# A mixture-of-experts kernel on one core: weight loads in units of 4 MB over groups of four slots, and one shared scatter for the last two experts

## The chip, the core and the metric

The kernel runs on one NeuronCore of a Trainium2 chip. Five engines work from queues of their own and meet through semaphores: TensorE (PE, matrix products), VectorE (DVE), ScalarE (ACT), GpSimd (POOL) and SyncE (SP, which here only issues transfers). 16 DMA engines move data between HBM and the on-chip memory SBUF. Each engine takes its instructions strictly in the order of its queue: an instruction that waits holds up all that stand behind it. The metric is the device time of one execution in microseconds, lower is better.

## The reference

One decoder layer on 256 tokens of width 1024, in float32: a mixer (a Mamba-2 branch and a gated MLP branch), cross-attention into 256 memory tokens, and a mixture of experts, each followed by a residual layer norm. The mixture of experts is what the change is about. The router picks 4 of 32 experts for each token; then for every expert

```
hgu  = xt @ w_gu[e] + b_gu[e]                 # 1024 x 2048 weights, 8 MB
gate = min(hgu[:, :1024], 7); up = clip(hgu[:, 1024:], -7, 7)
y    = ((up + 1) * gate * sigmoid(1.702 * gate)) @ w_down[e] + b_down[e]   # 1024 x 1024, 4 MB
acc += gates[:, e] * y
```

The weights of the experts are 32 x 12 MB = 384 MB, and each is read once.

## The kernel before

Phase A (mixer and attention) takes 20 or so slots of 1 MB in SBUF for its weights and intermediates. In phase B the experts follow one another, two experts to a pair. An expert takes at most 64 tokens. `gather` picks the tokens of a pair with a one-hot matrix (tile `pair`) into `xg` (a part of `cd`): four gathers per pair, each 8 matmuls into a PSUM buffer `sm` and two copies out, the first on ACT, the second on DVE. `gate_up` multiplies them with the 8 row blocks k of `w_gu` (eight instructions per k in the trace, four in the program) into two PSUM tiles `gu`, adds the bias with four short matmuls (line 1057) and then computes SwiGLU: DVE takes the minimum `gc` (line 1062), ACT the sigmoid `sg` (1063), DVE the clip (1064), the product (1065) and the last product `uc` (1066). `hidden_t` transposes `uc` by four matmuls (1075) into `sm`, and ACT copies the result to `hT` (1076). `down` multiplies `hT` with `w_down` (1089). After each odd expert `scatter` adds the weighted rows of the pair to `acc` (1100, 1105). PSUM tiles named `sm` have two buffers, which gathers, transposes, gate weights and scatters share.

What is issued when: the text of the kernel starts expert e+1 (its row blocks 0 and 1, `AHEAD = 2`) before the transposes of expert e. That is a wish, not the order: the instructions are put in order, engine by engine, by a scheduler at build time which estimates when each one's data will be there and takes what it holds to be ready first. So a change in the loads can change the order of the matmuls.

The weights of the experts come through SP's queue. `expert_w` gives each unit of the stream its slots: the first 22 loads of 1 MB go to slots as phase A gives them up (`FIRST`), then a ring of ten double slots (`RING`) takes units of 2 MB, of which a row (one partition's part) is 16384 bytes. A load waits until the matmuls that read its slots before are done. At the most 8 transfers are under way, since there are 8 semaphores for them.

At e = 14, 16 and 20 three pieces of other work are put between the experts: a table of overfull experts, `add_rest` (residual and bias rows, which also loads two small tiles `bd` through SP's queue) and the last norm's factors. At the end the last expert goes by column pieces: `scatter_one` adds expert 30 by itself (1116), then four `down_piece` (1124) with a `scatter_piece` each (1133) run for expert 31 with weights of its own (`weights_solo`), and `finish` normalizes and stores.

Of the kernel before, what the change touches and what calls it, by code (L numbers as in the profile page):

```python
# [8 lines left out]
F32 = mybir.dt.float32  # L9
# [8 lines left out]
P = 128  # L18
# [31 lines left out]
def block_kernel(ctx: ExitStack, tc: tile.TileContext, a, out):  # L50
# [11 lines left out]

    arena = cp.tile([P, len(SLOTS), 2048], F32, name="arena")
    big = ctx.enter_context(tc.tile_pool(name="big", bufs=1))

    def two(tag, dt=F32):

        return big.tile([P, 2, 2048], dt, tag=tag, name=uniq(tag))

# [133 lines left out]
    def w_parts():  # L203
        t = two(("t01", "t23")[tcount[0] % 2], F32R).rearrange("p q (i c) -> p q i c", i=2)
        tcount[0] += 1
        return [[t[:, q, i] for q in range(2)] for i in range(2)]
# [122 lines left out]
    kT = bt("e0").rearrange("p (k m) -> p k m", k=KB)  # L329
    mh, ml = feat("ab")  # L330
    hs, ls = w_parts()
# [30 lines left out]
    keys(2, wk2)  # L362
    xh, xl = feat("xhl")
    for k2 in range(4):
# [18 lines left out]

    gbm = bt("g").rearrange("p (g d) -> p g d", g=2)
    gvu = two("ab")
    gv = gvu[:, 0].rearrange("p (c d) -> p c d", c=2)
    st = stats_tile(2)
# [18 lines left out]
    ygh, ygl = feat("cd")  # L406
    uT = gvu[:, 1].rearrange("p (k t) -> p k t", k=KB)

# [190 lines left out]

    ysh, ysl = feat("ab")  # L600

# [79 lines left out]
    x1 = bt("h").rearrange("p (c d) -> p c d", c=2)  # L681
    mh, ml = feat("ab")
    mem = []
# [11 lines left out]
    proj_residual(hh, hl, x0, x1, st)  # L695
    xh, xl = feat("xhl")
    bg3 = bgs[:96, :].bitcast(BF16)
# [255 lines left out]
    class Pair:  # L953
# [36 lines left out]

        def weights_solo(self):

            G = self.gated()
            G2 = wk.tile([P, 2, 2, 2, CAP], F32, tag="t2", name="G2")
            pt = pst("sm", 2).rearrange("p (r c t) -> p r c t", r=2, c=2)
            for i in range(2):
                for c in range(2):
                    ve.tensor_copy(G2[:, i, c], G[:, c, i:i + 1, :].to_broadcast([P, 2, CAP]))
                    te.transpose(pt[:, i, c, :], G2[:, i, c].rearrange("p b s -> p (b s)"), ident)
            t = wk.tile([P, 2, 2, P], F32, tag="uy", name="PS")  # L1000
            se.activation(t, pt, AF.Copy)
            return [t[:, i] for i in range(2)]

    ucount = [0]

    def expert_w(src, apart=False):

        i = ucount[0]
        ucount[0] += 1
        if 2 * i < len(FIRST):  # L1010
            t = []
            for h in range(2):
                name = FIRST[2 * i + h]
                with tc.issue_after(wload[PHASE_A.index(FIRST_AFTER.get(name, ("wo", 3)))].ins):
                    if name in SLOTS:
                        t.append(bt(name))
                    elif name == "d":
                        t.append(cd[:, 1])
                    else:
                        if h == 0:  # L1020
                            both = two(name)
                        t.append(both[:, h])
                    nc.sync.dma_start(t[h], src[:, h])
            return t
        name = RING[(i - len(FIRST) // 2) % len(RING)]
        if name in SLOTS:
            at = SLOTS.index(name)
            t = arena[:, at:at + 2, :]
        else:
            t = two(name)  # L1030
        if apart:
            for h in range(2):
                nc.sync.dma_start(t[:, h], src[:, h])
        else:
            nc.sync.dma_start(t, src)
        return [t[:, h] for h in range(2)]

    def gate_up(src, sel, xe, before=None, last=False):

# [38 lines left out]

    def down(src, odd, hT, y, apart=False, between=None):

        for u in range(2):
            if u and between is not None:
                between()
            w = expert_w(src(u), apart)
            for b in range(4):
                k = 4 * u + b
                for n in range(2):
                    o = 64 * (n ^ odd)
                    te.matmul(y[n][o:o + 64, :], hT[:, b, 64 * u:64 * u + 64],  # L1089
                              w[b // 2][:, b % 2 * D + n * 512:b % 2 * D + (n + 1) * 512], start=(k == 0), stop=(k == KB - 1))  # L1090

# [14 lines left out]

    def scatter_one(y, PT):

        ys = wk.tile([P, 512], F32, tag="ux", name=uniq("ys"))
        se.activation(ys[0:64, :], y[0][0:64, :], AF.Copy)  # L1110
        ve.tensor_copy(ys[64:128, :], y[1][64:128, :])
        for n in range(2):
            o = slice(64 * n, 64 * n + 64)
            for c in range(2):
                ps = pst("sm", 2)
                te.matmul(ps, PT[o, c, :], ys[o, :], start=True, stop=True)
                av = acc[:, c, n * 512:(n + 1) * 512]
                ve.tensor_tensor(av, ps, av, ALU.add)

    def down_piece(hT, w, q):  # L1120
# [5 lines left out]
        ys = wk.tile([P, 512], F32, tag="ux", name=uniq("ys"))[:, :256]  # L1126
        se.activation(ys, y, AF.Copy)
        return ys

    def scatter_piece(ys, PT, q, st):  # L1130
        for c in range(2):
            ps = pst("sm", 2)[:, :256]
            te.matmul(ps, PT[:, c, :], ys, start=True, stop=True)
# [32 lines left out]
    def before(e, k):  # L1166
# [10 lines left out]
        if e % 2 and k % 2 == 0 and e < NE - 1:  # L1177
            pairs[e // 2 + 1].gather(k // 2)
        if e % 2 and k == 5 and e < NE - 1:
            p.weights()  # L1180

    def begin(e):
        xg = pairs[e // 2].xg
        current[e] = gate_up(lambda u: a["w_gu"][e, u], i96[:, e:e + 1], lambda k: xg[:, k, e % 2 * CAP:(e % 2 + 1) * CAP],
                             lambda k: before(e, k), e == NE - 1)

# [3 lines left out]
    for e in range(NE - 2):  # L1190
# [15 lines left out]
        if b == 0:  # L1206
            y = [pst(f"y{n}", 1) for n in range(2)]
        down(lambda u: a["w_down"][e, u], b, hT, y)
        if b:
# [10 lines left out]
    hT = hidden_t(uc)  # L1220
    PS = pairs[ea // 2].weights_solo()
    for k in range(AHEAD, KB):
# [3 lines left out]
    hTb = []  # L1226
    down(lambda u: a["w_down"][ea, u], 0, hT, y, True, lambda: hTb.append(hidden_t(uc)))
    scatter_one(y, PS[0])
    ys = None
    for q in range(4):  # L1230
        if q % 2 == 0:
            w = expert_w(a["w_last"][q // 2], True)
        new = down_piece(hTb[0], w[q % 2], q)
        if ys is not None:
            scatter_piece(ys, PS[1], q - 1, st)
        ys = new
    scatter_piece(ys, PS[1], 3, st)
    finish(st)
# [3 lines left out]
    with tc.For_i(0, nx, 1):  # L1242
# [35 lines left out]
        hT = hidden_t(swiglu())  # L1278
        down(lambda u: a["w_down"][bass.ds(ev, 1), u].rearrange("e p h d -> p (e h) d"), 0, hT, y)
        ys = wk.tile([P, 512], F32, tag="ux", name="ysx")  # L1280
# [11 lines left out]
        for i in range(2):  # L1292
# [8 lines left out]

FIRST = ["e1", "k", "g", "gb", "xhl", "xhl", "w3", "w4", "e0", "x0", "ab", "ab", "w5", "w0", "w1", "w2", "t01", "t01", "t23",
         "t23", "j", "d"]
SLOTS = ["e1", "k", "g", "gb", "w3", "w4", "e0", "x0", "w5", "w0", "w1", "w2", "j", "h"]
FIRST_AFTER = {"e1": ("z", 1), "k": ("wq", 0), "g": ("wq", 1), "gb": ("wo", 0)}

RING = FIRST[0:20:2]

# [15 lines left out]
def arrange(inputs):  # L1324
# [30 lines left out]
    wg, wd = I["w_gu"][0], I["w_down"][0]  # L1355
    r["w_gu"] = wg.reshape(NE, 4, 2, P, 2 * D).transpose(0, 1, 3, 2, 4)
    r["w_down"] = wd.reshape(NE, 2, 4, P, D).transpose(0, 1, 3, 2, 4).reshape(NE, 2, P, 2, 2 * D)
    r["w_last"] = wd[NE - 1].reshape(KB, P, 4, 256).transpose(2, 1, 0, 3).reshape(2, 2, P, 2 * D).transpose(0, 2, 1, 3)
    r["b_gu"], r["b_down"] = I["b_gu"][0], I["b_down"][0]
# [21 lines left out]
```

## Time and profile before

| | |
|---|---|
| median of 3 runs | 1318.44 us (1317.88 to 1318.74) |
| profiled execution | 1318.8 us, of which the span of its instructions 1317.1 us |
| PE busy | 1254.6 us (95%), DVE 451.4 us, ACT 315.6 us |
| read from HBM | 469.49 MB |
| first matmul of an expert | 393.62 us after the span's start |
| mean granted TensorE clock | 0.987 of full speed |

The profile page cuts the span into 40 slices of 33 us. A busy digit of 9 on PE says that matmuls were under way, not that they were dense. In the list of costliest groups and in the timelines `[2.08 <-DMA x]` says that the engine sat idle for 2.08 us before this group and that the landing of x ended it. A pair of experts is recognised by its scatter (line 1100); the time from one scatter to the next is what a pair costs.

### The profile page before, as it was taken

How to read it: one execution, taken by the hardware profiler on the slowest of the kernel's cores; microseconds unless marked ns; L12 is line 12 of the kernel's file. 1: busy time of each engine (PE TensorE's matmuls, PEld its weight loads, DVE VectorE, ACT ScalarE, POOL GpSimd, SP SyncE). 2: the span in 40 equal slices, each digit the busy share in tenths (PEclk: the TensorE clock that was granted, in tenths of full speed). 3: DMA queues.
4: the chain of work that ended last, by engine and by line, in shares of the span. 5: the costliest groups of instructions: out<-in, count | busy, mean ns of one | idle time of the engine just before them, and what ended most of it. 6: DMA issues, size and time to landing. Idle time of an engine off the chain costs nothing.

```text
span 1317.1 us, 15917 instructions
## 1 busy us (share of the span) xinstructions
PE 1254.6 (95%) x6767; PEld 686.7 (52%) x6768; DVE 451.4 (34%) x795; ACT 315.6 (24%) x536; POOL 28.6 (2%) x49
## 2 busy tenths in 40 slices
PE   6999999999999999999999999999999999989896
PEld 6899899989874343343333433333343433323232
DVE  4569766687441222121221122221221212202114
ACT  4746665544531111111111111101111111101000
POOL 2110000001000000000000000000000000000000
PEclk9999999999999999999999999969999999999998
DMA  9755543576789999999999999999999999999993
GB/s 356 242 175 195 192 160 133 193 289 225 277 315 362 422 425 428 427 427 428 427 427 428 429 428 427 412 427 427 426 429 428 427 428 426 427 427 428 429 421 134
DMA packets 43930, 472.00 MB, mean 358 GB/s; under 512 B 5104, under 2 KB 6928, under 8 KB 10064
## 3 DMA queue, kind: packets, MB, share of 16 engines
q1 hardware_dynamic: 39840, 464.41, 85.8%
q10 hardware_dynamic: 4016, 6.55, 1.6%
q8 instruction: 54, 0.88, 0.3%
q14 instruction: 20, 0.16, 0.0%
HBM read 469.49 MB, written 1.05 MB: 357 GB/s over the span
## 4 chain that ended last, share of the span: by engine, by line
PE 78%; DMA 15%; DVE 3%; ACT 2%; issue 1%; POOL 0%; ACTq 0%; DVEq 0%; SPq 0%; POOLq 0%
PE gu L1050 27%; PE y L1089 14%; PE mm L255 6%; PE mm L239 5%; PE mm L238 5%; PE mm L237 5%; PE sm L971 4%; PE sm L1100 4%; DMA arena<-in_w_down_dram 3%; DMA arena<-in_w_gu_dram 3%; DMA ab<-in_w_gu_dram 3%; DMA t<-in_w_gu_dram 3%; DMA t<-in_w_down_dram 2%; PE sm L1075 1%; DVE t L181 1%
## 5 line engine op out<-in xcount | busy, mean ns | idle before, releaser
L1050 PE MATMUL gu<-arena,cd 128*64 128x512 f32 x1240 | 279.8, 594 | 4.5 <-DMA arena<-in_w_gu_dram 4.5
L1050 PEld LDWEIGHTS gu<-arena,cd 128*64 128x64 f32 x1240 | 86.6, 137 | 171.2 <-issue 157.4
L181 DVE TENSOR_TENSOR t<-arena,t 128x1024 fp32r<-128x1024 f32 (+1 forms) x111 | 131.9, 1210 | 49.6 <-ACT t L180 49.6
L1089 PE MATMUL y<-arena,hT 128*64 128x512 f32 x592 | 140.4, 615 | 5.6 <-ACT hT L1076 5.6
L180 ACT ACTIVATE t<-arena 128x1024 fp32r<-128x1024 f32 (+1 forms) x114 | 113.9, 1039 | 59.1 <-issue 18.5
L1062 DVE TENSOR_SCALAR gc<-gu 128x512 f32<-128x512 f32 x32 | 22.1, 692 | 297.3 <-PE gu L1057 297.3
L237 PE MATMUL mm<-xhl,t 128*128 128x256 f32 x384 | 110.5, 288 | 0.0
L239 PE MATMUL mm<-xhl,t 128*128 128x256 f32 x384 | 108.9, 283 | 1.5 <-DVE t L181 1.5
L238 PE MATMUL mm<-xhl,t 128*128 128x256 f32 x384 | 108.7, 283 | 0.0
L1063 ACT ACTIVATE sg<-gc 128x512 f32<-128x512 f32 x32 | 20.2, 630 | 341.7 <-DVE gc L1062 341.7
L975 DVE TENSOR_SCALAR cd<-sm,par 128x128 f32<-128x128 f32 x64 | 26.2, 410 | 210.5 <-ACT cd L973 210.2
L1105 DVE TENSOR_TENSOR cd<-sm,cd 128x512 f32<-128x512 f32 x56 | 38.7, 692 | 170.9 <-PE sm L1100 170.9
L1050 PE MATMUL gu<-t,cd 128*64 128x512 f32 x384 | 87.1, 595 | 0.0
L1089 PEld LDWEIGHTS y<-arena,hT 128*64 128x64 f32 x592 | 42.5, 140 | 84.4 <-issue 74.8
L973 ACT ACTIVATE cd<-sm,par 128x128 f32<-128x128 f32 x64 | 29.3, 457 | 227.4 <-PE sm L971 226.0
L971 PEld LDWEIGHTS sm<-pair,arena 128*128 128x128 f32 x512 | 62.0, 191 | 31.7 <-issue 27.2
L239 PEld LDWEIGHTS mm<-xhl,t 128*128 128x128 f32 x384 | 73.5, 192 | 1.7 <-DVE t L181 1.7
L971 PE MATMUL sm<-pair,arena 128*128 128x128 f32 x512 | 71.3, 285 | 3.2 <-ACT pair L989 1.8
L238 PEld LDWEIGHTS mm<-xhl,t 128*128 128x128 f32 x384 | 73.6, 192 | 0.2
L237 PEld LDWEIGHTS mm<-xhl,t 128*128 128x128 f32 x384 | 73.5, 192 | 0.2
L1100 PE MATMUL sm<-ys,pair 128*128 128x512 f32 x120 | 59.1, 615 | 10.4 <-ACT ys L1094 10.2
L1050 PE MATMUL gu<-ab,cd 128*64 128x512 f32 x208 | 48.8, 613 | 4.0 <-DMA ab<-in_w_gu_dram 4.0
(320 smaller groups left out, 1432.6 us busy)
## 6 DMA issues: line engine op xcount, KB each, us to landing
arena<-in_w_gu_dram SPq DMA_DIRECT2D x71, 2048.0 KB, 32.3
arena<-in_w_down_dram SPq DMA_DIRECT2D x35, 2048.0 KB, 30.2
arena<-in_wa_dram SPq DMA_DIRECT2D x56, 1024.0 KB, 5.0
t<-in_w_gu_dram SPq DMA_DIRECT2D x22, 2048.0 KB, 35.1
ab<-in_w_gu_dram SPq DMA_DIRECT2D x13, 2048.0 KB, 31.5
xhl<-in_w_gu_dram SPq DMA_DIRECT2D x12, 2048.0 KB, 30.1
t<-in_w_down_dram SPq DMA_DIRECT2D x12, 2048.0 KB, 30.9
arena<-in_w_gu_dram SPq DMA_DIRECT2D x13, 1024.0 KB, 7.3
```

The lines of the kernel that those rows point to most:

```text
L180: se.activation(h, src, AF.Copy)
L181: sub_op[0] = (eng or ve).tensor_tensor(l, src, h.bitcast(F32), ALU.subtract)
L237: te.matmul(ps[:, b, :], wh, xh[:, k, :], start=(k == 0), stop=False)
L238: te.matmul(ps[:, b, :], wh, xl[:, k, :], start=False, stop=False)
L239: te.matmul(ps[:, b, :], wl, xh[:, k, :], start=False, stop=(k == KB - 1))
L255: last[0] = te.matmul(res[c], x[:, k, c * P:(c + 1) * P], w[k // 2 % 2][:, k % 2, :], start=(k == 0 and i == 0), stop=(k == KB - 1 and i = ...
L971: te.matmul(pg[:, b, :], x2[:, c, k * P:(k + 1) * P], self.t[:, 0, c, :], start=(c == 0), stop=(c == 1))
L973: se.activation(self.xg[:, k, :], pg[:, 0, :], AF.Identity, bias=b2[:, k:k + 1], scale=g2[:, k:k + 1])
L1050: te.matmul(t[64 * j:64 * j + 64, :], xe(k), ws[k][:, n * D + j * 512:n * D + (j + 1) * 512], start=(k == 0), stop=False)
L1089: te.matmul(y[n][o:o + 64, :], hT[:, b, 64 * u:64 * u + 64], w[b // 2][:, b % 2 * D + n * 512:b % 2 * D + (n + 1) * 512], start=(k == 0), ...
L1100: te.matmul(ps, PT[:, c, :], ys[n], start=True, stop=True)
L1105: ve.tensor_tensor(av, ps, av, ALU.add)
```

## The change

Three things are altered. First the slots: eight of the one-megabyte slots that phase A uses as pairs (`xh`, `xl`, `a`, `b` and `t0` to `t3`) become two tiles of four, two intermediates of phase A move to other slots (`h` and `j`), and the order of the first slots and of the ring changes so that the ring is five groups of four. Second the units: from expert 4 on a load brings four slots at once (4 MB, rows of 32768 bytes); experts 0 to 3 keep 2 MB, the last expert's second half of `w_gu` and expert 30's `w_down` come in units of 2 MB, the last `w_down` in four of 1 MB. The first half of the next expert's `w_gu` is now asked for as one unit. Third the end: `scatter_one` and `weights_solo` go; the pieces of expert 31 are written into the upper half of the tile `ys` that holds expert 30's rows in its lower half (ACT copies one half of the PSUM piece, DVE adds the other), and one `scatter_piece` per column piece serves both experts.

```
-RING = FIRST[0:20:2]
+RING = [8, 0, 12, 4, 16]
+NRING = 4 * len(RING)
...
+    def expert_w(src, n=1):
+        out = []
+        h = src.shape[1]
+        while len(out) < h:
+            i = ucount[0]
+            if i < len(FIRST):
+                m, name = 1, FIRST[i]
...
+            else:
+                m = min(n, h - len(out))
+                at = (rcount[0] + NRING - len(FIRST) % 4) % NRING
+                rcount[0] += m
+                t = slots(RING[at // 4] + at % 4, m)
+            ucount[0] += m
+            with after:
+                nc.sync.dma_start(t, src[:, len(out):len(out) + m])
...
-            if k % 2 == 0:
-                ws[k], ws[k + 1] = expert_w(src(k // 2), last and k == KB - 2)
+            if k % 4 == 0:
+                ws.update(enumerate(expert_w(src(k // 4), n_rows[k // 4]), k))
...
-    def down(src, odd, hT, y, apart=False, between=None):
+    def down(src, odd, hT, y, rows=4, between=None):
+        w = expert_w(src, rows)
+        for k in range(KB):
+            if k == 4 and between is not None:
                 between()
...
-        se.activation(ys, y, AF.Copy)
-        return ys
+        t = ys[q // 2][64:128, q % 2 * 256:q % 2 * 256 + 256]
+        se.activation(t, y[0:64, :], AF.Copy)
+        ve.tensor_tensor(t, y[64:128, :], t, ALU.add)
...
+    def rows_of(e):
+        return (2, 2) if e < 4 else (4, 4)
...
-    PS = pairs[ea // 2].weights_solo()
-    scatter_one(y, PS[0])
+    ve.tensor_copy(ys[0][0:64, :], y[0][0:64, :])
+    se.activation(ys[1][0:64, :], y[1][64:128, :], AF.Copy)
+    PT = pairs[ea // 2].PT
+    w = expert_w(a["w_last"])
```

PE's order around the SwiGLU of an odd expert (here 27) in the kernel before: the last bias matmul (1057), two row blocks of the next expert's gate-up, the four transposes of `uc`, the first matmul of `down`.

```order
L1057 MATMUL gu_6749<-bgs,i_109 64x512
L1050 MATMUL gu_6862<-ab_6864,cd_3791 64x512 x2
L1050 MATMUL gu_6863<-ab_6864,cd_3791 64x512 x2
L1050 MATMUL gu_6862<-ab_6864,cd_3791 64x512 x2
L1050 MATMUL gu_6863<-ab_6864,cd_3791 64x512 x2
L1075 MATMUL sm_6875<-ident,uc_6856 128x128 x4
L1089 MATMUL y_14_6774<-arena,hT_6874 64x512
```

The same place in the changed kernel (lines 1055, 1048, 1073 and 1085 are those matmuls; expert 25):

```order
L1055 MATMUL gu_6359<-bgs,i_109 64x512
L1073 MATMUL sm_6479<-ident,uc_6461 128x128
L1048 MATMUL gu_6467<-four_2_3788,cd_3731 64x512 x2
L1048 MATMUL gu_6468<-four_2_3788,cd_3731 64x512 x2
L1048 MATMUL gu_6467<-four_2_3788,cd_3731 64x512 x2
L1048 MATMUL gu_6468<-four_2_3788,cd_3731 64x512 x2
L1073 MATMUL sm_6479<-ident,uc_6461 128x128 x3
L1048 MATMUL gu_6467<-four_2_3788,cd_3731 64x512 x2
L1048 MATMUL gu_6468<-four_2_3788,cd_3731 64x512 x2
L1048 MATMUL gu_6467<-four_2_3788,cd_3731 64x512 x2
L1048 MATMUL gu_6468<-four_2_3788,cd_3731 64x512 x2
L1085 MATMUL y_13_6383<-arena,hT_6478 64x512
```

The first transpose has moved up to stand right behind the bias; the row blocks that stood between them stand behind it, and there are four of them instead of two before `down`. It is so for experts 4, 5, 30 and all odd ones from 7 to 29 (at 17 and 30 all four transposes stand there).

PE's order at an even expert (28) before, from the bias to the first matmul of `down`; 971 are gathers of the next pair, 988 the gate weights:

```order
L1057 MATMUL gu_6863<-bgs,i_109 64x512
L1050 MATMUL gu_6960<-arena,cd_3791 64x512 x2
L1050 MATMUL gu_6961<-arena,cd_3791 64x512 x2
L1050 MATMUL gu_6960<-arena,cd_3791 64x512 x2
L1050 MATMUL gu_6961<-arena,cd_3791 64x512 x2
L1075 MATMUL sm_6979<-ident,uc_6954 128x128 x4
L971 MATMUL sm_7006<-pair_6932,arena 128x128 x4
L971 MATMUL sm_7022<-pair_6932,arena 128x128 x4
L988 MATMUL sm_7038<-ident,G_7035 128x128 x2
L1089 MATMUL y_15_6985<-xhl_6987,hT_6978 64x512
```

The same place in the changed kernel (expert 26; 980 are the gathers):

```order
L1055 MATMUL gu_6468<-bgs,i_109 64x512
L980 MATMUL sm_6561<-pair_6532,arena 128x128 x4
L1073 MATMUL sm_6578<-ident,uc_6553 128x128 x4
L980 MATMUL sm_6603<-pair_6532,arena 128x128 x4
L980 MATMUL sm_6618<-pair_6532,arena 128x128 x3
L1048 MATMUL gu_6559<-arena,cd_3731 64x512 x2
```

Here one gather is left between the bias and the transposes, and further gathers stand right behind the transposes. It is so for the 12 even experts from 6 to 28.

DVE's order over the SwiGLU of an even expert in the changed kernel (1060 minimum, 1062 clip, 1063 product, 1064 last product, 984 the copy of the gather):

```order
L1060 TENSOR_SCALAR gc_5924<-gu_5840 128x512
L1062 TENSOR_SCALAR uc_5926<-gu_5841 128x512
L1063 TENSOR_TENSOR gc_5924<-gc_5924,sg_5925 128x512
L984 TENSOR_SCALAR cd_3731<-sm_5934,par 128x128
L1064 SCALAR_TENSOR_TENSOR uc_5926<-uc_5926,gc_5924 128x512
```

The copy of that gather stands ahead of the operation that ends `uc`; before it stood ahead of the minimum.

## Rows read from the trace of the kernel before

**Rows 1.** The page's 40 slices: PE busy tenths, granted clock tenths, GB/s moved.
```profile
PE   6999999999999999999999999999999999989896
...
PEclk9999999999999999999999999969999999999998
...
GB/s 356 242 175 195 192 160 133 193 289 225 277 315 362 422 425 428 427 427 428 427 427 428 429 428 427 412 427 427 426 429 428 427 428 426 427 427 428 429 421 134
```
**Rows 2.** Groups by line, 508 to 1073 us: busy, mean ns, idle before.
```profile
L1050 PE MATMUL gu<-arena,cd 128*64 128x512 f32 x768 | 172.3, 594 | 0.0
```
**Rows 3.** The chain of waits: start, us, what.
```profile
719.40 1.98 PE sm L1100 x4
...
773.30 1.98 PE sm L1100 x4
...
1104.33 38.82 DMA t<-in_w_gu_dram
```
**Rows 4.** PE's waits, 508 to 1290 us: total us, times, longest.
```profile
PE y L1089 <- ACT hT L1076: 9.0, 13, 0.7
...
PE gu L1050 <- DMA arena<-in_w_gu_dram: 4.5, 6, 1.2
PE gu L1050 <- DMA ab<-in_w_gu_dram: 4.0, 3, 2.1
PE sm L971 <- ACT pair L989: 1.8, 3, 0.6
PE y L1089 <- DMA t<-in_w_down_dram: 1.5, 2, 1.2
```
**Rows 5.** Timeline of one expert, 724 to 750 us: start, us, instructions.
```profile
726.87 1.16 PE L971 MATMUL sm<-pair,arena 128*128 128x128 f32 x8
...
728.07 0.46 ACT L973 ACTIVATE cd<-sm,par 128x128 f32<-128x128 f32 x1 [7.50 <-PE sm L971]
728.56 0.41 DVE L975 TENSOR_SCALAR cd<-sm,par 128x128 f32<-128x128 f32 x1 [4.08 <-ACT cd L973]
...
734.88 0.60 PE L1057 MATMUL gu<-bgs,i 96*64 96x512 bf16 x4
...
735.31 0.69 DVE L1062 TENSOR_SCALAR gc<-gu 128x512 f32<-128x512 f32 x1 [6.33 <-PE gu L1057]
735.32 3.60 PE L1050 MATMUL gu<-ab,cd 128*64 128x512 f32 x16
...
737.42 0.69 DVE L1066 SCALAR_TENSOR_TENSOR uc<-uc,gc 128x512 f32<-128x512 f32 x1
...
738.85 0.66 PE L1075 MATMUL sm<-ident,uc 128*128 128x128 f32 x4
```
**Rows 6.** Timeline of PE near the end, 1240 to 1310 us.
```profile
1271.98 3.65 PE L1050 MATMUL gu<-ab,cd 128*64 128x512 f32 x16 [1.50 <-DMA ab<-in_w_gu_dram]
...
1278.90 0.60 PE L1057 MATMUL gu<-bgs,i 96*64 96x512 bf16 x4
...
1282.34 0.63 PE L1075 MATMUL sm<-ident,uc 128*128 128x128 f32 x4 [0.88 <-DVE uc L1066]
...
1289.55 3.89 PE L1116 MATMUL sm<-ys,PS 64*128 64x512 f32 x8 [0.73 <-ACT ys L1110]
```
**Rows 7.** Timeline of PE, 1160 to 1182 us.
```profile
1167.65 3.65 PE L1050 MATMUL gu<-arena,cd 128*64 128x512 f32 x16 [1.23 <-DMA arena<-in_w_gu_dram]
...
1173.82 5.35 PE L1050 MATMUL gu<-ab,cd 128*64 128x512 f32 x16 [2.08 <-DMA ab<-in_w_gu_dram]
```
**Rows 8.** Stretches: us, busy (count) of PE, PEld, DVE, ACT, POOL; PEclk, DMA share, GB/s.
```profile
1175.00:1180.00 5.00, 4.76 (x18) 1.44 (x14) 0.00 (x0) 0.20 (x1) 0.00 (x0) 0.74 1.01 429
...
860.00:865.00 5.00, 5.00 (x22) 3.62 (x20) 1.36 (x4) 0.00 (x0) 0.00 (x0) 0.50 0.99 415
```
**Rows 9.** Stretches with 2-MB loads alone, then 1-MB loads alone.
```profile
1236.00:1262.00 26.00, 23.00 (x100) 7.74 (x100) 3.42 (x6) 2.38 (x4) 0.00 (x0) 1.00 1.00 427
1268.00:1286.00 18.00, 15.61 (x76) 5.06 (x72) 2.67 (x4) 1.23 (x2) 0.00 (x0) 1.00 1.01 421
```

More of the change, by code (lines that the diff above doesn't have):

```diff
@@ L64, in block_kernel, with fours @@
     big = ctx.enter_context(tc.tile_pool(name="big", bufs=1))
+    four = {}
+    def fours(i, dt):
+        if (i, dt) not in four:
+            four[i, dt] = big.tile([P, 4, 2048], dt, tag=f"four{i}", name=uniq(f"four{i}"))
+        return four[i, dt]
     def two(tag, dt=F32):
-        return big.tile([P, 2, 2048], dt, tag=tag, name=uniq(tag))
+        if tag == "cd":
+            return big.tile([P, 2, 2048], dt, tag=tag, name=uniq(tag))
+        at = SLOTS_R.index(tag)
+        return fours(at // 4, dt)[:, at % 4:at % 4 + 2, :]
     def bt(tag, shape=(P, 2048)):
@@ L203, in w_parts @@
     def w_parts():
-        t = two(("t01", "t23")[tcount[0] % 2], F32R).rearrange("p q (i c) -> p q i c", i=2)
+        t = two(("t0", "t2")[tcount[0] % 2], F32R).rearrange("p q (i c) -> p q i c", i=2)
         tcount[0] += 1
@@ L362, in block_kernel @@
     keys(2, wk2)
-    xh, xl = feat("xhl")
+    xh, xl = feat("xh")
     for k2 in range(4):
@@ L384, in block_kernel @@
     gbm = bt("g").rearrange("p (g d) -> p g d", g=2)
-    gvu = two("ab")
-    gv = gvu[:, 0].rearrange("p (c d) -> p c d", c=2)
+    gv = bt("h").rearrange("p (c d) -> p c d", c=2)
     st = stats_tile(2)
@@ L681, in block_kernel @@
     x1 = bt("h").rearrange("p (c d) -> p c d", c=2)
-    mh, ml = feat("ab")
+    mh, ml = feat("a")
     mem = []
@@ L695, in block_kernel @@
     proj_residual(hh, hl, x0, x1, st)
-    xh, xl = feat("xhl")
+    xh, xl = feat("xh")
     bg3 = bgs[:96, :].bitcast(BF16)
@@ L989, in weights @@
             se.activation(self.PT, pt, AF.Copy)
[L991 to L1002, printed above, removed]
@@ L1004, in block_kernel @@
-    ucount = [0]
[L1006 to L1036, printed above, removed]
@@ L1038, in gate_up, with slots @@
-    def gate_up(src, sel, xe, before=None, last=False):
+    ucount = [0]
+    rcount = [0]
+    def slots(i, n):
+        if i < len(SLOTS_R):
+            return fours(i // 4, F32)[:, i % 4:i % 4 + n, :]
+        i -= len(SLOTS_R)
+        return arena[:, i:i + n, :]
+    def expert_w(src, n=1):
[5 more added lines that the diff above has]
+                m, name = 1, FIRST[i]
+                if name == "d":
+                    t = cd[:, 1:2]
+                else:
+                    t = slots((SLOTS_R + SLOTS).index(name), 1)
+                after = tc.issue_after(wload[PHASE_A.index(FIRST_AFTER.get(name, ("wo", 3)))].ins)
+            else:
+                m = min(n, h - len(out))
+                at = (rcount[0] + NRING - len(FIRST) % 4) % NRING
+                assert at % m == 0
+                rcount[0] += m
+                t = slots(RING[at // 4] + at % 4, m)
+                after = ExitStack()
+            ucount[0] += m
+            with after:
+                nc.sync.dma_start(t, src[:, len(out):len(out) + m])
+            out += [t[:, q] for q in range(m)]
+        return out
@@ L1040, in gate_up @@
+    def gate_up(src, sel, xe, before=None, n_rows=(4, 4)):
         gp, up = pst("gu", 4), pst("gu", 4)
@@ L1077, in hidden_t @@
         return hT
-    def down(src, odd, hT, y, apart=False, between=None):
-        for u in range(2):
-            if u and between is not None:
+    def down(src, odd, hT, y, rows=4, between=None):
+        w = expert_w(src, rows)
+        for k in range(KB):
+            if k == 4 and between is not None:
                 between()
[L1084 to L1090, printed above, removed]
+            for n in range(2):
+                o = 64 * (n ^ odd)
+                te.matmul(y[n][o:o + 64, :], hT[:, k % 4, 64 * (k // 4):64 * (k // 4) + 64],
+                          w[k // 2][:, k % 2 * D + n * 512:k % 2 * D + (n + 1) * 512], start=(k == 0), stop=(k == KB - 1))
     def scatter(y, PT, first=False):
@@ L1105, in scatter, with down_piece @@
                     ve.tensor_tensor(av, ps, av, ALU.add)
[L1107 to L1120, printed above, removed]
+    def down_piece(hT, w, q, ys):
         y = pst(f"y{q % 2}", 1)[:, :256]
@@ L1132, in scatter_piece @@
             ps = pst("sm", 2)[:, :256]
-            te.matmul(ps, PT[:, c, :], ys, start=True, stop=True)
+            te.matmul(ps, PT[:, c, :], ys[q // 2][:, q % 2 * 256:q % 2 * 256 + 256], start=True, stop=True)
             av = acc[:, c, q * 256:q * 256 + 256]
@@ L1178, in before @@
             pairs[e // 2 + 1].gather(k // 2)
-        if e % 2 and k == 5 and e < NE - 1:
+        if e % 2 and k == 5:
             p.weights()
+    def rows_of(e):
+        return (2, 2) if e < 4 else (4, 4)
     def begin(e):
@@ L1184, in begin @@
         current[e] = gate_up(lambda u: a["w_gu"][e, u], i96[:, e:e + 1], lambda k: xg[:, k, e % 2 * CAP:(e % 2 + 1) * CAP],
-                             lambda k: before(e, k), e == NE - 1)
+                             lambda k: before(e, k), (4, 2) if e == NE - 1 else rows_of(e))
     begin(0)
@@ L1207, in block_kernel @@
             y = [pst(f"y{n}", 1) for n in range(2)]
-        down(lambda u: a["w_down"][e, u], b, hT, y)
+        down(a["w_down"][e], b, hT, y, rows_of(e)[0])
         if b:
@@ L1226, in block_kernel @@
     hTb = []
-    down(lambda u: a["w_down"][ea, u], 0, hT, y, True, lambda: hTb.append(hidden_t(uc)))
-    scatter_one(y, PS[0])
-    ys = None
-    for q in range(4):
[L1231 to L1237, printed above, removed]
+    down(a["w_down"][ea], 0, hT, y, 2, lambda: hTb.append(hidden_t(uc)))
+    ys = [wk.tile([P, 512], F32, tag="ux", name=uniq("ys")) for n in range(2)]
+    ve.tensor_copy(ys[0][0:64, :], y[0][0:64, :])
+    se.activation(ys[1][0:64, :], y[1][64:128, :], AF.Copy)
+    PT = pairs[ea // 2].PT
+    w = expert_w(a["w_last"])
+    for q in range(4):
+        down_piece(hTb[0], w[q], q, ys)
+        if q:
+            scatter_piece(ys, PT, q - 1, st)
+    scatter_piece(ys, PT, 3, st)
     finish(st)
@@ L1278, in block_kernel @@
         hT = hidden_t(swiglu())
-        down(lambda u: a["w_down"][bass.ds(ev, 1), u].rearrange("e p h d -> p (e h) d"), 0, hT, y)
+        down(a["w_down"][bass.ds(ev, 1)].rearrange("e p h d -> p (e h) d"), 0, hT, y)
         ys = wk.tile([P, 512], F32, tag="ux", name="ysx")
@@ L1355, in arrange @@
     wg, wd = I["w_gu"][0], I["w_down"][0]
-    r["w_gu"] = wg.reshape(NE, 4, 2, P, 2 * D).transpose(0, 1, 3, 2, 4)
-    r["w_down"] = wd.reshape(NE, 2, 4, P, D).transpose(0, 1, 3, 2, 4).reshape(NE, 2, P, 2, 2 * D)
-    r["w_last"] = wd[NE - 1].reshape(KB, P, 4, 256).transpose(2, 1, 0, 3).reshape(2, 2, P, 2 * D).transpose(0, 2, 1, 3)
+    r["w_gu"] = wg.reshape(NE, 2, 4, P, 2 * D).transpose(0, 1, 3, 2, 4)
+    r["w_down"] = wd.reshape(NE, KB, P, D).transpose(0, 2, 1, 3).reshape(NE, P, 4, 2 * D)
+    r["w_last"] = wd[NE - 1].reshape(KB, P, 4, 256).transpose(1, 2, 0, 3).reshape(P, 4, 2 * D)
     r["b_gu"], r["b_down"] = I["b_gu"][0], I["b_down"][0]
```

13 lines of the change are left out of this document (6 added, 7 removed).

## The prediction

> **What bounds the kernel now.** I read the page's slices first [rows 1]: through the expert stage PE shows nines, the granted clock stays at nine tenths or more except in two slices, and the 16 DMA engines bring 425 to 429 GB/s in nearly every slice. Two resources are full at once, so the question is which of them waits for the other. The groups by line give the first half of the answer: between 508 and 1073 us the 768 gate-up matmuls from `arena` had no idle time ahead of them at all [rows 2]. The chain gives the second: one scatter begins at 719.40 us, the next at 773.30, so a pair costs PE 53.9 us, and the first transfer on the chain stands at 1104.33 [rows 3]. A pair's weights are 2 x 12 MB = 25.17e6 bytes, 58.8 us at 428 GB/s. PE is thus 4.9 us per pair quicker than its loads; it lives on the slots that were full when it began, meets the loads near 1104 us, and from there they keep step. What PE then loses is small: of its waits between 508 and 1290 us the three on loads sum to 4.5 + 4.0 + 1.5 = 10.0 us, and the largest of all is the copy of `hT`, 13 times, 9.0 us [rows 4]. So PE has hardly any idle time in which something new could hide. A wait that the change puts into PE's queue at every expert adds to the end; one that it takes away can return 10 us by loads and 9 by `hT`, no more.
>
> **The change part by part.** *The transposes.* In the changed order of PE they stand right behind the bias, where two gate-up blocks stood before. PE takes its queue in order, so there it waits for `uc`, and behind the waiting transpose are queued the next expert's row blocks, which have their data and can't pass. How long the wait is, the trace shows at one expert in the middle and one at the end. In the middle the bias begins at 734.88, SwiGLU's minimum `gc` at 735.31, and the last operation begins at 737.42 and takes 0.69 us, so `uc` is done at 738.11; meanwhile PE ran two blocks in 3.60 us and found `uc` ready [rows 5]. Near the end the bias begins at 1278.90 and its matmuls end about 0.43 us later, at 1279.33; the transposes begin at 1282.34, after a wait on `uc` [rows 6]. From bias to transposes the chain therefore needs 3.0 us (2.8 in the first row, plus the signal). For 15 experts (4, 5, 30 and odd 7 to 29) nothing stands between: 15 x 3.0 = 45 us. For the 12 even ones from 6 to 28 one gather does, but its DVE copy of 0.41 us [rows 5] now stands ahead of the last operation of `uc`. The gather takes some 1.1 us, so 12 x (3.0 + 0.4 - 1.1) = 28 us. Together +73 us. Experts 0 to 3 stay as they are.
>
> *What follows the transposes.* Row blocks now stand between them and `down`, so the wait for `hT` goes: -9.0 us [rows 4]. At even experts several gathers come in a row, with two `sm` buffers for them; each waits for the copies of an earlier one. No row shows it. From below nothing, if matmuls cover it; from above 12 x (0.46 + 0.41) = 10.4 us, ACT's and DVE's copy [rows 5]. I take the middle, +5, since some gate-weight matmuls lie between.
>
> *Loads.* With PE later by more than 2 us per expert, its waits on loads go: -10.3 us (10.0 [rows 4] and 0.3 of a small one in the same list). The rate with 32768-byte rows is not shown. 8192-byte rows gave 421 GB/s, 16384-byte rows 427 [rows 9]. From nothing to half of that step again, 0.7%, is some 5 us over the 384 MB; slower by as much is possible if a unit starts later because all four slots have to be free. Either way I cost it at 0: what hides it is the full slots, which PE would no longer use up. The Trainium skill, in "DMA: Bandwidth & Descriptors", section "Anatomy of one DMA", gives a transfer some 2.0 us of fixed cost plus its bytes at 436 GB/s; by that an estimate for one alone is 308 GB/s with 2 MB and 361 with 4 MB, a large gain from larger units. The trace disagrees: 2-MB units already move 427 GB/s [rows 9], as several are under way.
>
> *The tail.* `scatter_one` goes, 3.89 us and 0.73 of waiting [rows 6]; a DVE addition per piece comes in, of which only the last is on the path, +0.6 by the DVE rows of the same kind of tile [rows 5]; the extra weight transposes save 0.3 by estimate from the four of 0.66 [rows 5]. Sum -4.3 us.
>
> *The first slots.* Phase A's loads change order and two intermediates move. No row prices that: 4 us either way, costed at 0.
>
> *`add_rest`.* There PE runs at half clock [rows 8], from 860 to 865 us, for about 20 us, which costs 10. Denser row blocks there may shorten it: 0 to -10, I take -5.
>
> **The clock.** A PE that waits may lose its clock. After a wait of 2.08 us sixteen gate-up matmuls took 5.35 us, where 3.65 is normal [rows 7]; the granted clock was 0.74 of full in the five microseconds around [rows 8], that is, part of the stretch at 1.2 GHz in place of 2.4. After waits of 1.23 [rows 7] and 1.50 us [rows 6] the same matmuls took 3.65: no fall. The new waits are 2.3 and 3.0 us, longer than the one that cost 5.35 - 3.65 = 1.7 us. Bounds: nothing (dense work between the waits keeps the clock), and all 27 x 1.7 = 46 us. I take the 15 long ones and a few of the others, 18 x 1.7 = +31 us, and take off the one fall of before that goes with its load, -1.7.
>
> [...]
>
> **The sum.** +73 - 9 + 5 - 10.3 - 4.3 - 5 + 31 - 1.7 = +79 us. The profiled execution took 1318.8 us, 0.4 above the median of the runs, so 1318.8 + 78.7 - 0.4 = about 1397. A pair would cost 53.9 + 5.3 for the stalls, some 0.4 for gathers, -0.7 for `hT` and 2.6 for the clock: 61.5 us. That is longer than its loads' 58.8, so the DMA engines would no longer be full, near 25.17e6 / 61.5 = 409 GB/s.
>
> **Rivals.** *The clock holds.* The stalls come, but after dense matmuls none of them lowers the clock. For it: waits of 1.23 and 1.50 us didn't. Against: 2.08 did, and the new ones are longer. 1397 - 31 = 1366 us; if the stalls are also somewhat shorter than the chain, 1350.
>
> *The larger units starve PE.* A 4-MB unit waits for four slots in place of two, and a matmul for a unit of which it needs a quarter. For it: PE did end without a lead, with waits on loads of up to 2.1 us [rows 4]. Against: with the stalls a pair of PE is at least as long as its loads, so the lead stays. If it came, one unit's 4.19e6 bytes at 428 GB/s, 9.8 us, once or twice beside the forecast: about 1410.
>
> *The stalls are nearly empty* (the other side). If PE's waits came to 1.1 us or less per expert, 27 x 1.1 = 30, they would be paid by what goes (9 + 10.3 + 4.3 + 5 + 1.7 = 30): that is the point from which it turns. It would take a chain of SwiGLU shorter by 1.9 us, for instance because DVE and ACT read PSUM more quickly while PE stands still. At 0.9 us the time is 1318.4 + 24 - 30 = 1312. Against: from 735.31 to 738.11 there are four DVE operations of 0.69 us, 2.8 us in all, with no gap [rows 5]; each would have to be three times as fast.
>
> *The order gains nothing and loses nothing*: no such case has a mechanism; it lies only where that rival ends between.
>
> **How the numbers follow.** Chances: forecast 0.72 (its own range 1380 to 1418), the clock holds 0.18 (1350 to 1380), starving 0.04, empty stalls 0.04, the rest 0.02. The range 1352 to 1420 holds all but the edges and the last three cases. What a measurement of this kernel can tell from no change is about 0.2%, 2.6 us. Slower by more than that: 0.93; faster 0.04; within it 0.03.
>
> **What would show it.** PE's waits would be led by the transposes' `sm` on DVE `uc`, some 27 times and 73 us. Scatter to scatter would be 59 us (clock holds) to 62. The clock's digits would fall below nine all through the expert stage, and GB/s to 405 to 425; PE's waits on loads and on `hT` would be near nothing, and `scatter_one` gone from the end. The forecast is wrong if the transposes wait for less than 1.1 us on the mean, if the clock stays full (then 1366), or if PE still waits for loads.

## The result and the profile after

The changed kernel took 1375.28 us (median of 5 runs, 1370.49 to 1376.96) beside 1318.74 for the kernel before: a ratio of 1.041, 95% interval 1.040 to 1.043, so 4.1% slower. The forecast was 1397 us, range 1352 to 1420. The profiled execution is the quickest of the five, 1370.49 us (span 1368.8); it accounts for 51.7 of the 56.5 us.

The page's slices of the kernel after: busy tenths of PE, granted clock, DMA share, GB/s. They answer to [rows 1].

```profile
PE   7999999999999998899998989998999989889996
...
PEclk9999999999999999999999999899999999999998
DMA  9746544584888899999999998499999999999960
GB/s 367 247 162 212 189 135 163 204 301 175 337 353 373 363 429 429 432 431 432 433 427 421 413 434 370 188 437 433 429 429 414 429 428 413 430 411 423 406 256 32
```

PE shows eights where it showed nines. The rate still stands near 430 GB/s in most slices but falls to 413 and 406 in others and to 188 in one: the loads now wait for PE and no longer PE for them. The clock's digit stays at nine in every slice of the stage but one, where the prediction looked for digits below nine all through it; a fall lasts a few microseconds, a slice 34. Over the middle of the stage (us; busy and count of PE, PEld, DVE, ACT, POOL; PEclk, DMA share, GB/s) it is

```profile
508.00:1073.00 565.00, 510.50 (x2348) 195.97 (x2349) 106.29 (x215) 59.07 (x112) 0.00 (x0) 0.97 0.96 410
```

The waits of PE in the kernel after, from 391 us to the end (engine, line, what it waited for: total us, times, longest), which answer to [rows 4]; lines 1073, 1096 and 980 are the transposes, the scatter and the gather:

```profile
PE sm L1073 <- DVE uc L1064: 62.6, 27, 2.7
PE sm L1096 <- ACT ys L1090: 10.3, 15, 0.7
PE sm L980 <- ACT pair L998: 7.7, 13, 0.6
PE sm L980 <- DVE pair L972: 1.0, 1, 1.0
...
PE sm L980 <- ACT hT L1074: 0.6, 1, 0.6
...
```

The first row did not lead the list before; it is there 27 times. The rows of [rows 4] on loads, and that of `down` on `hT`, are gone.

One odd and one even expert in PE's timeline of the kernel after (start us, us, instructions, idle before and what ended it), to be set beside [rows 5]:

```profile
726.32 0.60 PE L1055 MATMUL gu<-bgs,i 96*64 96x512 bf16 x4
729.66 0.33 PE L1073 MATMUL sm<-ident,uc 128*128 128x128 f32 x1 [2.74 <-DVE uc L1064]
729.92 5.35 PE L1048 MATMUL gu<-arena,cd 128*64 128x512 f32 x16
...
746.88 3.96 PE L1096 MATMUL sm<-ys,pair 128*128 128x512 f32 x8 [0.69 <-ACT ys L1090]
750.77 7.09 PE L1048 MATMUL gu<-four,cd 128*64 128x512 f32 x32
757.69 0.60 PE L1055 MATMUL gu<-bgs,i 96*64 96x512 bf16 x4
758.22 1.16 PE L980 MATMUL sm<-pair,arena 128*128 128x128 f32 x8
761.17 0.66 PE L1073 MATMUL sm<-ident,uc 128*128 128x128 f32 x4 [1.79 <-DVE uc L1064]
```

The odd expert waits 2.74 us, the even one 1.79 behind its gather. After the first of these waits sixteen gate-up matmuls take 5.35 us in place of 3.65; after the second everything runs at full speed. The even expert two before it waited for as long and lost its clock:

```profile
699.33 0.94 PE L1073 MATMUL sm<-ident,uc 128*128 128x128 f32 x4 [1.79 <-DVE uc L1064]
700.06 3.12 PE L980 MATMUL sm<-pair,arena 128*128 128x128 f32 x14
```

And the odd expert behind the first two waited 2.75 us and kept its clock:

```profile
789.99 0.33 PE L1073 MATMUL sm<-ident,uc 128*128 128x128 f32 x1 [2.75 <-DVE uc L1064]
790.25 3.65 PE L1048 MATMUL gu<-arena,cd 128*64 128x512 f32 x16
```

So the length of the last wait alone does not decide it. Of the 27 waits 13 were followed by half speed: 9 of the 15 of about 2.7 us and 4 of the 12 of about 1.8. What decides it, no run here shows. The odd and the even expert shown first, in stretches (columns as above):

```profile
724.00:734.00 10.00, 7.26 (x29) 2.27 (x27) 2.67 (x4) 0.63 (x1) 0.00 (x0) 0.83 0.99 417
756.00:766.00 10.00, 8.21 (x52) 4.62 (x50) 3.72 (x8) 2.09 (x4) 0.00 (x0) 1.00 1.01 436
```

0.83 says that about a third of that stretch was granted 1.2 in place of 2.4 GHz.

The chain of waits in the kernel after, three scatters (to [rows 3]):

```profile
685.04 1.98 PE sm L1096 x4
...
746.88 1.98 PE sm L1096 x4
...
805.51 1.98 PE sm L1096 x4
```

These pairs cost 61.8 us, with two falls of the clock in it, and 58.6, where one cost 53.9; 61.5 was forecast with the clock's share and 59 without.

### The profile page after: what moved, and what is told of

Same layout as the page of the kernel before. It is cut to its first block, busy times and chain, and to the rows that moved or that the text cites. A ratio compares the mean times of both kernels' runs of the same rounds, so it can differ in the third digit from the quotient of the medians.

```text
span 1368.8 us, 15770 instructions
## 1 busy us (share of the span) xinstructions
PE 1262.2 (92%) x6757; PEld 692.2 (51%) x6758; DVE 448.7 (33%) x791; ACT 321.2 (23%) x536; POOL 29.5 (2%) x49
## 4 chain that ended last, share of the span: by engine, by line
PE 90%; DVE 5%; ACT 3%; issue 1%; DMA 0%; ACTq 0%; DVEq 0%
PE gu L1048 35%; PE y L1085 16%; PE mm L265 8%; PE mm L248 5%; PE mm L249 5%; PE mm L247 5%; PE sm L1096 4%; PE sm L980 4%; PE sm L1073 2%; DVE gc L1060 1%; DVE gc L1063 1%; DVE uc L1064 1%; ACT sg L1061 1%; PE sm L946 1%; ACT ys L1090 1%; PE gu L1055 1%
## 5 line engine op out<-in xcount | busy, mean ns | idle before, releaser
L1048 PE MATMUL gu<-arena,cd 128*64 128x512 f32 x1240 | 288.1, 608 | 0.0
L1048 PE MATMUL gu<-four,cd 128*64 128x512 f32 x800 | 193.5, 629 | 0.0
L191 DVE TENSOR_TENSOR four<-arena,four 128x1024 fp32r<-128x1024 f32 (+1 forms) x119 | 137.8, 1168 | 82.7 <-ACT four L190 75.4
L190 ACT ACTIVATE four<-arena 128x1024 fp32r<-128x1024 f32 (+1 forms) x122 | 122.2, 1014 | 103.0 <-PE mm L248 49.0
L247 PE MATMUL mm<-four,four 128*128 128x256 f32 x496 | 142.2, 287 | 0.0
L248 PE MATMUL mm<-four,four 128*128 128x256 f32 x496 | 140.5, 283 | 0.0
L249 PE MATMUL mm<-four,four 128*128 128x256 f32 x496 | 140.5, 283 | 0.0
L1085 PE MATMUL y<-arena,hT 128*64 128x512 f32 x576 | 127.3, 594 | 0.0
L1048 PEld LDWEIGHTS gu<-four,cd 128*64 128x64 f32 x800 | 57.9, 143 | 112.2 <-issue 109.6
L247 PEld LDWEIGHTS mm<-four,four 128*128 128x128 f32 x496 | 95.1, 192 | 0.2
L248 PEld LDWEIGHTS mm<-four,four 128*128 128x128 f32 x496 | 95.1, 192 | 0.2
L249 PEld LDWEIGHTS mm<-four,four 128*128 128x128 f32 x496 | 95.0, 192 | 0.0
L1085 PE MATMUL y<-four,hT 128*64 128x512 f32 x416 | 93.0, 594 | 0.0
L1073 PE MATMUL sm<-ident,uc 128*128 128x128 f32 x128 | 24.7, 300 | 62.6 <-DVE uc L1064 62.6
## 6 DMA issues: line engine op xcount, KB each, us to landing
arena<-in_w_gu_dram SPq DMA_DIRECT2D x33, 4096.0 KB, 17.4
```

Of the source, the lines that this page charges most:

```text
L190: se.activation(h, src, AF.Copy)
L191: sub_op[0] = (eng or ve).tensor_tensor(l, src, h.bitcast(F32), ALU.subtract)
L247: te.matmul(ps[:, b, :], wh, xh[:, k, :], start=(k == 0), stop=False)
L248: te.matmul(ps[:, b, :], wh, xl[:, k, :], start=False, stop=False)
L249: te.matmul(ps[:, b, :], wl, xh[:, k, :], start=False, stop=(k == KB - 1))
L1073: te.transpose(pt[:, f, :], uc[:, f * P:(f + 1) * P], ident)
```

## Experiments

The kernel before ran beside each group of four and took 1319.42 us (median) beside the first four and 1320.01 beside the second.

**The usual order with 4-MB units.** Is it the order or the size of the units?

```diff
...
-        for f in range(4):
-            te.transpose(pt[:, f, :], uc[:, f * P:(f + 1) * P], ident)
+        with ExitStack() if then is None else tc.issue_after(then.ins):
+            for f in range(4):
+                te.transpose(pt[:, f, :], uc[:, f * P:(f + 1) * P], ident)
...
-            current[e + 1][0](k)
-        hT = hidden_t(uc)
+            mm = current[e + 1][0](k)
+        hT = hidden_t(uc, mm)
...
```

> The changed kernel with one thing put back: the four transposes of uc are held until the next expert's row blocks 0 and 1 are issued, so on PE two gate-up blocks stand again between the bias and the transposes; units of 4 MB, slots and the shared scatter stay. Theory (the order costs): the 27 waits on uc, 62.6 us in the changed kernel, go to under 3 us, the clock stays up outside add_rest, PE meets its loads again, and the time is set by the stream and the shorter tail: 1308 to 1318 us. Rival (units of 4 MB cost by themselves, by starving PE): stays above 1340 us with PE waiting for loads.

1314.03 us (1313.69 to 1314.71), 0.9959 of before, interval 0.9944 to 0.9973: 61 us less than the changed kernel, from the order alone. The theory holds for the order and the time. PE's waits, 391 us to the end (line 1087 is `down`):

```profile
...
PE gu L1048 <- DMA arena<-in_w_gu_dram: 6.3, 3, 2.2
PE gu L1048 <- DMA four<-in_w_gu_dram: 4.9, 4, 2.0
PE y L1087 <- DMA arena<-in_w_down_dram: 4.6, 4, 2.0
...
PE y L1087 <- DMA four<-in_w_down_dram: 2.5, 3, 1.9
...
```

No wait on `uc` is left and PE meets its loads again. The rival was wrong in its place and its price: the 4-MB units do let PE wait, but for 18 us in all. One part of the theory fails: the clock does not stay up outside `add_rest`. Five of the eight waits on loads of 1.86 to 2.19 us are followed by half speed.

**The usual order with 2-MB units.**

```diff
-        return (2, 2) if e < 4 else (4, 4)
+        return (2, 2)
```

> The changed kernel with units of 2 MB (16384-byte rows) for all experts; new slots and the shared scatter stay. The order of PE is by this the same as in the run with the transposes held back, so the two differ only in the size of a unit. Theory (the order costs, the unit size nothing): waits on uc under 3 us and the time within 3 us of that run, 1308 to 1318 us. Rival 1 (larger rows are faster): 3 to 6 us more than with 4 MB. Rival 2 (4-MB units starve PE): clearly less than that run.

1320.77 us (1319.56 to 1321.91), 1.0008 of before, interval 0.9998 to 1.0019. This is 6.7 us more than with 4 MB, outside the theory's range: rival 1 is right, the larger units are faster, by slightly more than its 3 to 6 us. The stretch from 508 to 1073 us, in the runs with 4-MB, 2-MB and (below) 1-MB units, each in its own fence:

```profile
508.00:1073.00 565.00, 543.24 (x2559) 209.77 (x2559) 113.82 (x229) 63.64 (x121) 0.00 (x0) 0.99 1.00 430
```
```profile
508.00:1073.00 565.00, 539.40 (x2557) 207.13 (x2553) 115.46 (x231) 64.62 (x121) 0.00 (x0) 1.00 1.01 427
```
```profile
508.00:1073.00 565.00, 539.18 (x2531) 202.49 (x2529) 115.16 (x229) 63.95 (x121) 0.00 (x0) 1.00 1.01 420
```

430 against 427 GB/s is 0.7%, 6 us over the 900 or so that the stream lasts. This kernel also answers why the order moved at all: only the size of the units differs from the changed kernel, and the scheduler, which estimates when a load will be there, puts the row blocks ahead of the transposes again by itself, at all experts but one. Expert 30 keeps its early transposes:

```profile
PE sm L1073 <- DVE uc L1064: 2.7, 1, 2.7
```

PE waits for loads again behind that place, so it does not set the end. Against the kernel before, which has units of 2 MB as well, this run gains nothing, though its tail is shorter and its first gate-up matmul begins at 390.14 us in place of 393.62. The loads of the first experts take that back, as the run with another order of the first slots shows below.

**Early transposes with 2-MB units.** Early transposes as in the changed kernel, without its units. All four now stand right behind the bias at every expert from 4 to 30, so the order is not quite that of the changed kernel, which has a gather between at the even experts:

```diff
...
-        return (2, 2) if e < 4 else (4, 4)
+        return (2, 2)
...
+        if e >= 4:
+            before(e + 1, 0)
+            hT = hidden_t(uc)
         for k in range(AHEAD):
-            current[e + 1][0](k)
-        hT = hidden_t(uc)
+            current[e + 1][0](k, tr[-4] if e >= 4 else None, e >= 4)
...
```

Here the gate-up products of those two row blocks are issued after `tr[-4]`, the first transpose.

> Units of 2 MB as in the run before, but all four transposes of uc are forced to stand right behind the bias for experts 4 to 30, ahead of the next expert's row blocks. Theory (the order costs): 27 waits of 2.7 us each, 73 us, less some 20 us of waits on loads and on hT that go, plus about 12 for the clock: 1370 to 1385 us although no unit is larger than 2 MB. Rival (the larger units are what costs): within 10 us of the run with 2-MB units and the usual order.

1384.6 us (1383.39 to 1386.53), 1.050 of before: as the theory had it, 64 us above the run with the same units. PE's first row of waits:

```profile
PE sm L1076 <- DVE uc L1065: 74.3, 27, 2.8
```

**The same with PE kept busy.**

```diff
...
+        with tc.issue_after(bias[-1].ins):
+            for _ in range(fill):
+                te.matmul(pt, onesB, onesB[:, 0:1].to_broadcast([P, 512]), start=True, stop=True)
...
```

> The run with forced early transposes, with 12 short bf16 matmuls added into the transposes' own PSUM buffer ahead of them, about 2.6 us of work without use, so that PE does not stand still while it waits for uc. Theory (the waits cost their length, and beside it the clock falls after some of them): the time between bias and transposes stays, the granted clock falls only around add_rest, and the time is 10 to 20 us under the run without them. Rival (the falls have another cause): the same count of half-clock stretches and the same time within 3 us. If the filler is longer than the wait: more, by 27 times the excess.

1348.79 us (1348.65 to 1349.78): 36 us less, more than the 10 to 20 expected. The cost of the clock was underrated. One expert without the filler, and the same expert with it:

```profile
669.39 0.60 PE L1056 MATMUL gu<-bgs,i 96*64 96x512 bf16 x4
672.82 0.63 PE L1076 MATMUL sm<-ident,uc 128*128 128x128 f32 x4 [2.83 <-DVE uc L1065]
```
```profile
660.01 0.60 PE L1056 MATMUL gu<-bgs,i 96*64 96x512 bf16 x4
660.54 2.79 PE L1080 MATMUL sm<-onesB 128*128 128x512 bf16 x12
663.36 0.66 PE L1083 MATMUL sm<-ident,uc 128*128 128x128 f32 x4
```

From bias to transposes it is 3.43 and 3.35 us, the same. What goes is the clock that fell afterwards: the mean granted clock rises from 0.974 to 0.997.

**The changed kernel with PE kept busy.** The same filler on 4-MB units, 12 matmuls or, behind a gather, 8. The four transposes are held together behind it and ahead of the next row blocks; in the changed kernel one or four of them stand there.

> The changed kernel with its early transposes and 4-MB units, and short bf16 matmuls without use between the bias and the transposes (12 where the transposes follow the bias, 8 where a gather stands between). The transposes are held behind these and the next row blocks behind the first transpose. Theory (the waits cost their length and also the clock): the 13 half-clock stretches of the expert stage, 48 us, go, and half of that comes back: 1375 - 24 = 1351 us, 1346 to 1358. Rival (only the net difference to the kernel before, 48 - 24 us of half clock, is the cost of the waits; the other stretches have their own cause): 1363 us. Rival 2 (the filler only takes the place of the waits): 1375.

1342.76 us (1342.07 to 1343.57): 32.5 us less than the changed kernel, more than any of the three had. Gate-up matmuls in the changed kernel and in this one, 391 to 1390 us (busy us, mean ns, idle before):

```profile
L1048 PE MATMUL gu<-arena,cd 128*64 128x512 f32 x1232 | 286.3, 608 | 0.0
L1048 PE MATMUL gu<-four,cd 128*64 128x512 f32 x800 | 193.5, 629 | 0.0
```
```profile
L1049 PE MATMUL gu<-arena,cd 128*64 128x512 f32 x1238 | 279.2, 595 | 0.0
L1049 PE MATMUL gu<-four,cd 128*64 128x512 f32 x800 | 179.0, 595 | 0.0
```

21.6 us of the difference are gate-up matmuls that run faster. The theory took half of the time at half clock as one profiled execution showed it; that execution was the quickest of its kernel, 4.8 us under the median, and lost less to the clock (mean 0.980) than the others (0.975 to 0.979). Against its own 1370.49 the gain is 27.7.

**The shared scatter alone**, put into the kernel before (`scatter_one` and `weights_solo` taken out, the pieces as in the change).

> The kernel before with the third part of the change alone: no scatter_one, one shared scatter for the last two experts; units of 2 MB, slots and ring as before. Theory (scatter_one was on the path of the end): 1318.7 - 4.3 = 1314.4 us. Rival (PE would stand before the last pieces' loads anyway): within 1 us of before.

1318.19 us, 0.9984 of before, interval 0.9975 to 0.9993: 1.8 us less, between the two. The end of PE's timeline shows where the rest went (1112 and 1121 are a column piece and its scatter):

```profile
1289.47 1.95 PE L1112 MATMUL y<-t,hT 128*64 128x256 f32 x16 [0.81 <-DVE ys L1216]
1292.34 0.70 PE L1121 MATMUL sm<-ys,pair 128*128 128x256 f32 x2 [0.93 <-DVE ys L1116]
```

The pieces now wait for two copies of expert 30's rows, and each scatter piece for the addition of its halves, which did not exist before. PE's order is not that of the changed kernel either: there two column pieces stand ahead of the first scatter, so that it does not wait. The 1.8 us are thus not what this part is worth in the changed kernel.

**Another order of the first slots.**

```diff
-FIRST = [..., "w1", "w2", "j", "w3", "w4", "t0", "t1", "t2", "t3", "d"]
+FIRST = [..., "w1", "w2", "t0", "t1", "t2", "t3", "w3", "w4", "j", "d"]
```

> The run with 4-MB units and the transposes held back, and beside it the first slots in another order: t0 to t3 ahead of w3, w4 and j, so that the ring asks for slots in the order in which the first experts give them up. Theory (the stream lost time at 420 to 430 and 450 to 460 us, where its next unit waited for t1 although w3 and w4 were free; 272 and 264 GB/s there, some 7 us): the gaps close and the time is 1307 to 1311 us. Rival (in phase A, loads of w3 and w4 now wait behind those of t0 to t3, and what is gained is lost there): 1313 to 1316 us.

1314.32 us (1313.46 to 1314.81), the same as without the edit. The theory falls, and so does the rival's reason, for the gaps between 420 and 460 us did not close: 247 and 208 GB/s in the two stretches of 10 us from 420 and 450, where 272 and 264 had been. Between 385 and 490 us SP waited for gate-up blocks ahead of loads into their slots, up to 17.4 us at a time without the edit and 20.0 with it; which slot is asked for first did not shorten that. The kernel before has no such gaps:

```profile
420.00:430.00 10.00, 10.00 (x51) 3.63 (x47) 0.41 (x1) 0.46 (x1) 0.00 (x0) 1.00 1.01 433
...
450.00:460.00 10.00, 9.98 (x38) 3.41 (x40) 3.16 (x6) 1.02 (x2) 0.00 (x0) 1.00 0.99 418
```

The run with 2-MB units, on the new slots, has them too (238 and 203 GB/s). So they come with the new slots, or the new way of asking for loads, and not with the 4-MB units, and by 490 us that run has moved about 2.4 MB less than the kernel before, 5 to 6 us of the stream by estimate (258 against 263 GB/s over 490 us). Which of the two does it, no run separates.

**Units of 1 MB** in the usual order, `(1, 1)` for `(4, 4)`.

> The run with the transposes held back and units of 1 MB (8192-byte rows) from expert 4 on in place of 4 MB. Theory (with the usual order the stream sets the end, and a unit's rows set its rate: 431 GB/s with 32768-byte rows, 428 with 16384, 421 with 8192 by the last loads of the kernel before): 384 MB less the first loads take 1.6% longer than with 2 MB, 14 us: 1333 to 1337 us. Rival (the rate hangs on the number of transfers under way and not on rows; or the smaller units free slots earlier and gain that back): within 4 us of the run with 2-MB units, 1317 to 1325.

1335.37 us (1334.73 to 1335.98), 1.0114 of before, inside the theory's range; the third row above has the rate, 420 GB/s. With the usual order the stream sets the end, and the size of a unit sets the stream. The number of transfers under way does not: loads of 1, 2 and 4 MB landed 19.8, 39.1 and some 37 us after their issue (medians), which at these rates makes about 8, 8 and 4 of them at a time by estimate. Whether it is the length of a row or the bytes of a unit, which change together here, no run separates.

So the best version measured is the change with its transposes held back: 1314.0 us, 5.4 under the kernel before. The 4-MB units are worth 6.7 us by themselves; the order that they brought about cost 61.

## Why the prediction was right, and where it was off

The mechanism was right and so was the sign. The bound (PE dense, no slack), the 27 waits on `uc`, the waits that go and the half-clock stretches behind the new waits are all in the trace, and undoing the order alone gives all of it back. The sum was 22 us too high against the median, 27 against the profiled execution. Measured by itself the forecast missed: 1375 lies below its own range of 1380 to 1418 and within that of the rival "the clock holds" (1350 to 1380), whose mechanism the trace refutes. That the stated range holds is owed to its reaching over both. Term by term, in the profiled execution:

- *The transposes*, +73: measured 62.6, less the 0.88 of before [rows 6], +62. It and the clock are the largest errors, both too dear. The 3.0 us rested on taking the end of the bias at 0.43 us after its start, where its own row says 0.60 [rows 6]; the direct wait is 2.74. Behind a gather it is 1.79, not 2.3: the gather's DVE copy was added in full, 0.41. It does stand in the chain, ahead of the last operation of `uc`, but from bias to transposes the even expert takes 3.48 us where the odd one takes 3.34, so the copy costs 0.14. DVE's operations overlap a little where they follow at once (the copy begins at 760.11, the product before it ends at 760.19), and the copy and the last operation take 0.32 and 0.61 us of the chain in place of 0.41 and 0.69:

```profile
758.84 0.64 ACT sg L1061
759.50 0.69 DVE gc L1063
760.19 0.32 DVE cd L984
760.51 0.61 DVE uc L1064
```

- *What follows*, -9 for `hT` and +5 for the gathers: -9.7, and +5.9 + 0.3 = +6.2 (7.7 on ACT's `pair` against 1.8 in [rows 4], and 1.0 on DVE's against 0.7). Right in size, though the gathers wait mostly for the gate weights' copy of `pair`, and not for their own two copies.
- *Loads*, -10.3: all gone. Right. That larger rows are worth nothing here was right as well, and the 0.7% taken as half a step was the measured one; it is worth 6 us only when PE waits for loads. That the trace disagrees with the estimate for one transfer alone, as the prediction has it, the trace can't say: at 32 us from issue to landing some 7 of the 2-MB loads were under way.
- *The tail*, -4.3: by the trace the first column piece follows `down` after a wait of 0.82 us, where `scatter_one` and its waits took 4.6 before, so -3.7. Right.
- *The first slots*, 0, 4 either way: the first gate-up matmul begins at 388.79 us, not 393.62 as before: -4.8. This lay beyond the bound.
- *The clock*, with `add_rest` 31 - 1.7 - 5 = +24: by the mean granted clocks, 0.980 over 1368.8 us and 0.987 over 1317.1, the two spent some 55 and 34 us at half speed (twice the missing share), so +10, and +15 at the clock of 0.976 that the other runs of the changed kernel had. The falls behind the new waits were fewer than the 18 taken: without some 9 us at the very end, where PE is done, and 7 at `add_rest`, 39 of the 55 us remain, 20 us lost, which is 12 times 1.7. `add_rest` went as taken, or better: of the 20 us at half speed about 7 are left in this stretch:

```profile
880.00:895.00 15.00, 12.89 (x55) 6.25 (x52) 6.02 (x12) 1.63 (x3) 0.00 (x0) 0.77 1.04 450
```

The sum of these, 62 - 9.7 + 6.2 - 10.3 - 3.7 - 4.8 + 10, is 50, against 51.7 measured.

In the example that the Trainium skill gives ("TensorE: Matmul & The Clock Gate", section "HAM oscillation"), every wait for a load, some 3 to 5 us long, makes the burst of matmuls behind it begin at half speed. The waits here are shorter, 1.79 to 2.75 us, and 13 of 27 had that effect, so the trace agrees only in part: shorter waits can do it too, and not each does. Its core is borne out: filling the waits alone brought the clock back, and 36 and 32.5 us with it.

The rivals: "the clock holds" (1366) lay close to the profiled execution by accident, for the clock did fall: it took the stalls as too long and the clock at nothing, and the two errors cancel. Starving did not show: no wait on a load is left in the changed kernel. Empty stalls did not come: the last operation of `uc` begins 2.59 us after the bias with PE idle (at 728.91) and 2.60 after it with PE busy with filler (at 662.61). The rate was foretold at 409 GB/s and is 410 over the middle of the stage. That it is so near is luck: the loads run near 430 in most slices, and without the 14 us of a hole that the last section explains the mean would be 420 by estimate.

## What to carry to other kernels

When an automatic scheduler orders an engine's queue, read the order of the built program after any change in loads: a 6.7-us gain in the stream was paid for with 61 us because transposes moved up past two blocks of independent work. A wait in a dense matmul engine costs more than its length when the clock falls after it; here about half as much again. And a faster stream gained nothing here once the engine that it feeds had been made the slower one: in the changed kernel PE waits for no load.

## What was not expected of the hardware

A few short bf16 matmuls without use in a wait of 2.7 us took 36 us off one kernel and 32.5 off another, at an unchanged length of the waits: the one remedy measured here for a wait that stays.

The hole in GB/s (188 in one slice) has another cause than the slots. SP's waits in the kernel after, 840 to 880 us, and the stretch that follows from them (columns as in the stretches above):

```profile
SPq L920 <- PE sm L1096: 30.5, 2, 28.9
```
```profile
857.00:871.00 14.00, 13.31 (x59) 4.35 (x55) 0.66 (x1) 2.38 (x4) 0.00 (x0) 1.00 0.00 1
```

The two small loads of `add_rest` (line 920) wait 28.9 us for a scatter to free their tile, and all loads of weights stand behind them in SP's queue. In the kernel before the same wait was there (its line 911):

```profile
SPq L911 <- PE sm L1100: 26.4, 2, 24.8
```

It left no more than a slice with 412 GB/s [rows 1], since the transfers already under way covered it: a load landed some 32 us after its issue there, and 17 to 20 us after it in the changed kernel (medians). In the changed kernel 14 us went by without a transfer, and PE, with full slots, did not notice.
